# An MLP of seven block products: VectorE is held to the order in which its operations are written

## The chip, the cores and the metric

The kernel runs on one core of a Trainium2 chip. The metric is the time of one execution on the device in microseconds; what counts is the median of several runs. The hardware profiler took one execution by itself, and all rows below are from that one.

## The reference

A decoder trunk of two layers on 1024 tokens with 1024 channels, in float32. Each layer has a mixer (layer 0 gated DeltaNet, layer 1 sliding-window attention), an MLP and a gated embedding:

```python
h = h + mix
h = h + conv_ffn(rmsnorm(h, norm_ffn[i]), f_w_up[i], f_conv[i], f_w_down[i])
gate = jax.nn.sigmoid(rmsnorm(h, norm_ple[i]) @ ple_w_gate[i])
h = h + gate * (p[i] @ ple_w_proj[i])
```

The MLP, which the change is about, has 2816 hidden channels and a causal depthwise convolution with three taps behind its up projection:

```python
def conv_ffn(x, w_up, conv_w, w_down):
    u = causal_dwconv(x @ w_up, conv_w)
    gate, val = u[..., :D_FF], u[..., D_FF:]
    return (jax.nn.silu(gate) * val) @ w_down
```

## The kernel before

Channels lie on the 128 partitions and tokens along the free dimension. Every matmul operand is a pair, a rounded high part and the rest as a low part, and a product is three matmuls: high by high, low by high, high by low. All matmuls have 512 columns here, half of the tokens.

**Chunks.** `ffn` works through the hidden channels in 22 chunks j of 128. One chunk has a gate row block `z1` (tile `zg`) and a value row block `z2` (`zv`), each for two halves of the tokens. These 2 x 2 blocks are made from seven products instead of eight, in the fixed order b11, t2, t3, t1, b21, t4, b22 (`up`, L1356), each 12 matmuls. The inputs `mix.x` (b11, t12, t34, x1) are made before. The weights are sums of raw tiles: `weights` (L1240) makes s1, s2, s3 (L1252, L1253, L1255) and the second s2 (L1260) on VectorE; ScalarE rounds each to its high part (L1233) and GpSimd takes the low part (L1234). `take` (L1268) keeps four products' weights ready ahead.

The products add up in three PSUM banks of the pool `mm`: p1 (b11, then b21 on top), p7 (t3, then t4 on top), p5 (t1, then b22 on top). p6 (t2) uses the pool `d`. VectorE reads a bank between its two products, so the second has to wait for that read: `dd` = p6 - p1 (L1377), then `zv` half 1 = p7 + dd (L1394, the p7 add), minus p5 (L1397), times the row factor `rb[1]` of the norm (L1398); after b21 `zg` half 0 (L1402, L1404); after t4 `zv` half 0 (L1407, L1409); after b22 `zg` half 1 (L1416, L1418).

**Gate.** `taps` is the convolution: one operation on ScalarE (L321) and two on VectorE (L323). The value taps of chunk j follow t4 in the same chunk. `gated` (L1305), called in the chunk behind, makes the gate taps, the Silu on ScalarE (L1307), the product with the value (L1308), and by `split` its high part on ScalarE (L250, `gh`) and its low part on VectorE (L251, `gl`). Both taps read all of `z1` or `z2`, so the next chunk's p7 add, which writes into `zv`, comes behind the value taps.

In chunk 1 the row factors come into being (`nrm.factor`, `nrm.banks`), and what chunk 0 left in `zv` and `zg` is scaled by them first (L1385), so that both convolutions of chunk 0 lie in chunk 1.

**Down steps.** `step` (L1343) is a piece of the down projection: 2 x 6 matmuls on two finished chunks into two banks of the pool `d`, which has three, and two additions into an `h` tile that is loaded from DRAM beforehand and goes back there (L1340, L1350, L1351). From chunk 3 on a chunk has four steps: behind b11, behind t2, behind t4 and behind b22. Chunk 1 has none, chunk 2 has the latter two.

**Order.** The program is recorded in the order in which it is written; a scheduler then puts each engine's instructions in an order by readiness as it estimates it. `pin = tc.keep_in_program_order` exempts an instruction from that: pinned instructions of one engine keep their written order. The wrapper `E` around TensorE pins all matmuls of these stages. VectorE (`V`), ScalarE (`A`) and GpSimd (`G`) are left to the scheduler, as are the DMAs on SP's queue.

Of the kernel before, what the change touches and what calls it, by code (L numbers as in the profile page):

```python
# [9 lines left out]
F32R = mybir.dt.float32r  # L10
AF = mybir.ActivationFunctionType
ALU = mybir.AluOpType
MUL, ADD, SUB, MAX = ALU.mult, ALU.add, ALU.subtract, ALU.max
# [64 lines left out]
class Slot:  # L78
# [7 lines left out]
    def f(self):  # L86
        return self.t[:, :].bitcast(F32)
# [22 lines left out]
def kernel(  # L110
# [20 lines left out]
    out: bass.AP,  # L131
):
    nc = tc.nc
    V, A, G = nc.vector, nc.scalar, nc.gpsimd

    cp = ctx.enter_context(tc.tile_pool(name="cp", bufs=1))
    sp = ctx.enter_context(tc.tile_pool(name="sp", bufs=1))
# [5 lines left out]
    ps_ = ctx.enter_context(tc.tile_pool(name="ps", bufs=2, space=PSUM))  # L143
    S = Slots(sp, NSLOT)
    pin = tc.keep_in_program_order

    class PE:


        pinned = False  # L150
# [169 lines left out]
    def conv(dst, z, w, taps, a=0, b=T):  # L320
        A.activation(dst[:, a:b], z[:, a:b], AF.Copy, scale=w[:, 0:1])  # L321
        for i in range(1, taps):
            V.scalar_tensor_tensor(dst[:, a:b], z[:, a + i:b + i], w[:, i:i + 1], dst[:, a:b], MUL, ADD)  # L323
# [891 lines left out]
    def ffn(l, mix, nxt):  # L1215
# [72 lines left out]
        z1, z2 = S.wide("zg"), S.wide("zv")  # L1288
# [6 lines left out]
        gs = {}  # L1295
        ys = {}
        rb = []

        def taps(m, z):
            y = S.get("yf")  # L1300
            o = m * CF
            conv(y, z, fcv[:, o:o + CF], CF)
            return y

        def gated(j):  # L1305
            y1, y2 = taps(2 * j, z1), ys.pop(j)
            A.activation(y1[:, :], y1[:, :], AF.Silu)  # L1307
            V.tensor_tensor(y1[:, :], y1[:, :], y2[:, :], MUL)  # L1308
            S.put(y2)
            gs[j] = split(y1, "g")  # L1310
            S.put(y1)

        def gated_last():
# [42 lines left out]
        def up(j, early, late):  # L1356
            last = j == NF - 1

            def done(n):
                if last:  # L1360
                    mix.put(n)

            if j == 0:
                p1, p6, p7, p5 = first
                A.copy(dd, p1)
                V.tensor_tensor(dd, p6, dd, SUB)
                V.tensor_tensor(zh(z2, 1), p7, dd, ADD)
                V.tensor_tensor(zh(z2, 1), zh(z2, 1), p5, SUB)
            else:
                p1 = pmt()  # L1370
                prod(p1, *take(), "b11")
                A.copy(dd, p1)
                for _ in range(early[0]):
                    step()
                p6 = pdt()
                prod(p6, *take(), "t2")
                V.tensor_tensor(dd, p6, dd, SUB)  # L1377
                if j == 1:
                    nrm.factor()
                    p7 = pmt()  # L1380
                    prod(p7, *take(), "t3")
                    rb.extend(nrm.banks())
                    for z in (z2, z1):
                        for h in range(2):
                            V.tensor_tensor(zh(z, h), zh(z, h), rb[h], MUL)  # L1385
                        if z is z2:
                            ys[0] = taps(1, z2)
                for _ in range(early[1]):
                    step()
                gated(j - 1)  # L1390
                if j > 1:
                    p7 = pmt()
                    prod(p7, *take(), "t3")
                V.tensor_tensor(zh(z2, 1), p7, dd, ADD)  # L1394
                p5 = pmt()
                prod(p5, *take(), "t1")
                V.tensor_tensor(zh(z2, 1), zh(z2, 1), p5, SUB)  # L1397
                V.tensor_tensor(zh(z2, 1), zh(z2, 1), rb[1], MUL)  # L1398
            done("b11")
            done("t2")  # L1400
            prod(p1, *take(), "b21", first=False)
            A.copy(zh(z1, 0), p1)  # L1402
            if j:
                V.tensor_tensor(zh(z1, 0), zh(z1, 0), rb[0], MUL)  # L1404
            prod(p7, *take(), "t4", first=False)
            done("t4")
            V.tensor_tensor(zh(z2, 0), p7, dd, ADD)  # L1407
            if j:
                V.tensor_tensor(zh(z2, 0), zh(z2, 0), rb[0], MUL)  # L1409
            for _ in range(late[0]):  # L1410
                step()
            if 0 < j < NF - 1:
                ys[j] = taps(2 * j + 1, z2)
            prod(p5, *take(), "b22", first=False)
            done("b22")
            V.tensor_tensor(zh(z1, 1), p5, dd, SUB)  # L1416
            if j:
                V.tensor_tensor(zh(z1, 1), zh(z1, 1), rb[1], MUL)  # L1418
            else:
                mix.sum_squares()  # L1420
            for _ in range(late[1]):
                step()
# [54 lines left out]
        for j in range(NF):  # L1477
            n = len(todo) + len(loaded)
            if j == 2:
                load_step()  # L1480
            if j < 2 or n == 0:
                early = late = (0, 0)
            elif j == 2:
                early, late = (0, 0), (1, 1)
            elif n == 2:
                early, late = (1, 1), (0, 0)
            else:
                early, late = (1, 1), (1, 1)
            up(j, early, late)
        S.put(sa, sb)  # L1490
        hT = []
        for m in range(KT):
# [219 lines left out]
```

## Time and profile before

| what | us |
|---|---|
| median of 3 runs (2741.79 to 2749.13) | 2745.27 |
| the profiled execution | 2740.68 |
| its span from first to last instruction | 2738.8 |
| TensorE busy in the span (96%) | 2640.8 |
| VectorE busy (65%) | 1792.9 |
| GpSimd busy (43%) | 1191.4 |
| ScalarE busy (41%) | 1114.9 |

The profile gives busy time by engine, waits by the instruction that ended them, and all instructions in order of time. A matmul of 512 columns is shown with about 0.39 us, but starts come 0.23 us apart, since matmuls overlap in the pipeline; a gap in TensorE's work is therefore best read from the distance of two starts. The granted clock is TensorE's, as a share of its upper level.

### The profile page before, as it was taken

Reading aid. Unit: us, or ns where it says so; the run is one execution under the profiler, and the core shown is the slowest. Engines: PE = TensorE matmul, PEld = TensorE weight load, DVE = VectorE, ACT = ScalarE, POOL = GpSimd, SP = SyncE. Lnnn points to the kernel's source line nnn. Section 1 sums busy time; section 2 is a strip of 40 time slices with the busy share of each in tenths; the row PEclk is TensorE's granted clock in tenths of the full one; section 3 lists DMA queues with packets and bytes.
Section 4 is the critical chain, followed back from the end, with each engine's and each line's share of the span. In section 5 each row is a group of like instructions: output and inputs, shape, how many; then the busy total and the mean of one; then the engine's idle time right before and its main releaser. Section 6 shows DMA issues by size and latency. Waiting matters only on the chain. (4 is left out here: it accounts for less than half of the span.)

```text
span 2738.8 us, 35465 instructions
## 1 busy us (share of the span) xinstructions
PE 2640.8 (96%) x12914; PEld 2130.2 (78%) x12914; DVE 1792.9 (65%) x2645; ACT 1114.9 (41%) x2176; POOL 1191.4 (43%) x1132
## 2 busy tenths in 40 slices
PE   9899999999999999999999999999999999999998
PEld 7788787878777887888778776667778888888786
DVE  6555555564787777677774437775877767677745
ACT  5443443442643333333353225554533333333443
POOL 4444443442554444444532323335644444444354
PEclk9999999999999999999999999999999999999999
DMA  5222211232325555555432221122255555554323
GB/s 176 89 73 58 67 55 56 67 95 78 109 84 187 181 182 180 203 198 181 161 117 71 90 59 49 46 92 100 81 187 187 182 191 178 199 198 167 103 93 110
DMA packets 167215, 340.85 MB, mean 124 GB/s; under 512 B 38912, under 2 KB 91648, under 8 KB 167040
## 3 DMA queue, kind: packets, MB, share of 16 engines
q1 hardware_dynamic: 166176, 337.20, 37.2%
q8 instruction: 102, 1.67, 0.3%
q10 hardware_dynamic: 864, 1.38, 0.1%
q14 instruction: 73, 0.60, 0.1%
HBM read 232.56 MB, written 99.68 MB: 121 GB/s over the span
## 5 line engine op out<-in xcount | busy, mean ns | idle before, releaser
L202 POOL TENSOR_TENSOR wlo<-wraw,whi 128x512 fp32r<-128x512 f32 (+1 forms) x204 | 269.8, 1340 | 380.6 <-ACT whi L199 344.1
L153 PE MATMUL mm<-xh,whi 128*128 128x512 f32 x856 | 356.2, 416 | 3.9 <-ACT xh L255 2.8
L153 PE MATMUL mm<-xh,wlo 128*128 128x512 f32 x856 | 347.9, 406 | 0.0
L153 PE MATMUL mm<-xl,whi 128*128 128x512 f32 x856 | 346.0, 404 | 0.8 <-DVE xl L256 0.8
L212 POOL TENSOR_TENSOR dlo<-draw,dhi 128x256 fp32r<-128x256 f32 (+1 forms) x160 | 163.1, 1020 | 332.9 <-ACT dhi L211 295.7
L1234 POOL TENSOR_TENSOR wlo<-wraw,whi 128x512 fp32r<-128x512 f32 x132 | 192.6, 1466 | 147.7 <-ACT whi L1233 145.4
L1234 POOL TENSOR_TENSOR wlo<-sa,whi 128x512 fp32r<-128x512 f32 x132 | 194.1, 1470 | 141.0 <-ACT whi L1233 141.0
L153 PE MATMUL d<-gh,dhi 128*128 128x512 f32 x576 | 228.7, 397 | 4.7 <-DVE h L1350 4.2
L153 PE MATMUL d<-gl,dhi 128*128 128x512 f32 x576 | 226.9, 394 | 0.7 <-DVE gl L251 0.7
L153 PE MATMUL d<-gh,dlo 128*128 128x512 f32 x576 | 227.3, 395 | 0.0
L1350 DVE TENSOR_TENSOR h<-h,d 128x512 f32<-128x512 f32 x288 | 193.1, 680 | 32.6 <-PE d L153 32.2
L199 ACT CAST whi<-wraw 128x1024 fp32r<-128x1024 f32 (+3 forms) x122 | 100.1, 822 | 238.5 <-PE mm L153 123.4
L153 PEld LDWEIGHTS mm<-xh,wlo 128*128 128x128 f32 x856 | 163.3, 191 | 33.6 <-POOL wlo L202 0.2
L153 PEld LDWEIGHTS mm<-xh,whi 128*128 128x128 f32 x856 | 163.6, 191 | 30.6 <-ACT xh L255 3.2
L153 PEld LDWEIGHTS mm<-xl,whi 128*128 128x128 f32 x856 | 163.5, 191 | 26.9 <-DVE xl L256 1.4
L153 PE MATMUL mm<-t34h,whi 128*128 128x512 f32 x352 | 139.4, 396 | 3.7 <-DVE zv L1394 3.0
L153 PE MATMUL mm<-t34l,whi 128*128 128x512 f32 x352 | 139.6, 397 | 3.2 <-POOL t34l L919 3.2
L153 PE MATMUL mm<-x1l,whi 128*128 128x512 f32 x352 | 138.9, 395 | 0.2 <-DVE x1l L919 0.2
L153 PE MATMUL mm<-x1h,whi 128*128 128x512 f32 x352 | 138.8, 394 | 0.0
L153 PE MATMUL mm<-t34h,wlo 128*128 128x512 f32 x352 | 138.7, 394 | 0.0
L323 DVE SCALAR_TENSOR_TENSOR yf<-zv,fcv,yf 128x1024 f32<-128x1024 f32 (+1 forms) x92 | 121.5, 1321 | 26.3 <-ACT yf L321 26.2
L153 PE MATMUL mm<-x1h,wlo 128*128 128x512 f32 x352 | 138.2, 392 | 0.0
(382 smaller groups left out, 6564.0 us busy)
## 6 DMA issues: line engine op xcount, KB each, us to landing
hf<-h SPq DMA_DIRECT2D x160, 512.0 KB, 3.3
h<-hf SPq DMA_DIRECT2D x160, 512.0 KB, 4.2
wraw<-f_up SPq DMA_DIRECT2D x88, 512.0 KB, 3.3
draw<-f_down SPq DMA_DIRECT2D x144, 128.0 KB, 2.1
wraw<-a_in SPq DMA_DIRECT2D x32, 512.0 KB, 3.5
wraw<-g_w SPq DMA_DIRECT2D x24, 512.0 KB, 3.3
row<-rowd SPq DMA_DIRECT2D x16, 512.0 KB, 3.7
wraw<-b_in SPq DMA_DIRECT2D x12, 512.0 KB, 3.6
```

Source lines behind the costliest of these rows:

```text
L153: i = nc.tensor.matmul(*a, **k)
L199: A.copy(hi, raw)
L202: G.tensor_tensor(lo[:, i:j], raw[:, i:j], hi[:, i:j].bitcast(F32), SUB)
L212: G.tensor_tensor(lo, raw, hi[:, :].bitcast(F32), SUB)
L323: V.scalar_tensor_tensor(dst[:, a:b], z[:, a + i:b + i], w[:, i:i + 1], dst[:, a:b], MUL, ADD)
L1234: G.tensor_tensor(lo, src, hi.bitcast(F32), SUB)
L1350: V.tensor_tensor(t[:, hs(h)], t[:, hs(h)], ps, ADD)
```

## The change

`V` becomes a wrapper like TensorE's. While `V.pinned` is set, from chunk 1 to the end of chunk 21, each VectorE operation keeps its written place. The MLP's code is written in another order for it: `gated` is cut into three pieces, the gate taps and Silu behind b11 (in chunk 1 behind the scaling), the product and its high part behind t2, the low part behind the second step. `gated_last`, the down projection behind it and chunk 0 are not pinned.

```diff
-    V, A, G = nc.vector, nc.scalar, nc.gpsimd
+    A, G = nc.scalar, nc.gpsimd
...
+    class Vector:
+        pinned = False
+        def __getattr__(self, name):
+            f = getattr(nc.vector, name)
+            return (lambda *a, **k: pin(f(*a, **k))) if self.pinned else f
+    V = Vector()
...
-        def gated(j):
-            y1, y2 = taps(2 * j, z1), ys.pop(j)
+        def gate_taps(j):
+            y1 = taps(2 * j, z1)
             A.activation(y1[:, :], y1[:, :], AF.Silu)
+            return y1
+
+        def gate_high(j, y1):
+            y2 = ys.pop(j)
             V.tensor_tensor(y1[:, :], y1[:, :], y2[:, :], MUL)
             S.put(y2)
-            gs[j] = split(y1, "g")
+            hi = S.get("gh", F32R)
+            A.copy(hi[:, :], y1[:, :])
+            return hi
+
+        def gate_low(j, y1, hi):
+            lo = S.get("gl", F32R)
+            gs[j] = hi, lo
+            V.tensor_tensor(lo[:, :], y1[:, :], hi.f(), SUB)
             S.put(y1)
...
                 A.copy(dd, p1)
+                if j > 1:
+                    y1 = gate_taps(j - 1)
                 for _ in range(early[0]):
                     step()
...
                             ys[0] = taps(1, z2)
+                    y1 = gate_taps(0)
+                gh = gate_high(j - 1, y1)
                 for _ in range(early[1]):
                     step()
-                gated(j - 1)
+                gate_low(j - 1, y1, gh)
...
+            V.pinned = j > 0
             up(j, early, late)
+        V.pinned = False
```

Two places on VectorE, as the built programs have them. A row gives the line, the operation, and the tile written with those read. After the change every pinned row carries the wrapper's line, L154. The first place is chunk 1 of the first layer, from the scaling on. `s_6532` and `s_6537` are the row factors in PSUM, `yf_243` the value taps, `yf_244` the gate taps and then the product, `mm_6514` is p7, `mm_6561` p5, `sb` holds dd, `sa` the weight sums. Before:

```order
L1385 TENSOR_TENSOR zg_192_5916<-zg_192_5916,s_6532 128x512
L1385 TENSOR_TENSOR zg_192_5916<-zg_192_5916,s_6537 128x512
L323 SCALAR_TENSOR_TENSOR yf_243_6544<-zv_193_5917,fcv_5912,yf_243_6544 128x1024
L1260 TENSOR_TENSOR sa_190_5914<-sa_190_5914,wraw_5954 128x512
L323 SCALAR_TENSOR_TENSOR yf_243_6544<-zv_193_5917,fcv_5912,yf_243_6544 128x1024
L323 SCALAR_TENSOR_TENSOR yf_244_6550<-zg_192_5916,fcv_5912,yf_244_6550 128x1024
L1394 TENSOR_TENSOR zv_193_5917<-mm_6514,sb_191_5915 128x512
L323 SCALAR_TENSOR_TENSOR yf_244_6550<-zg_192_5916,fcv_5912,yf_244_6550 128x1024
L1397 TENSOR_TENSOR zv_193_5917<-zv_193_5917,mm_6561 128x512
L1398 TENSOR_TENSOR zv_193_5917<-zv_193_5917,s_6537 128x512
L1308 TENSOR_TENSOR yf_244_6550<-yf_244_6550,yf_243_6544 128x1024
```

With the change, in the same place:

```order
L154 SCALAR_TENSOR_TENSOR yf_243_6544<-zv_193_5917,fcv_5912,yf_243_6544 128x1024 x2
L154 TENSOR_TENSOR zg_192_5916<-zg_192_5916,s_6532 128x512
L154 TENSOR_TENSOR zg_192_5916<-zg_192_5916,s_6537 128x512
L154 SCALAR_TENSOR_TENSOR yf_244_6550<-zg_192_5916,fcv_5912,yf_244_6550 128x1024 x2
L154 TENSOR_TENSOR yf_244_6550<-yf_244_6550,yf_243_6544 128x1024
L154 TENSOR_TENSOR gl_246_6558<-yf_244_6550,gh_245_6556 128x1024
L154 TENSOR_TENSOR zv_193_5917<-mm_6514,sb_191_5915 128x512
L154 TENSOR_TENSOR zv_193_5917<-zv_193_5917,mm_6561 128x512
L154 TENSOR_TENSOR zv_193_5917<-zv_193_5917,s_6537 128x512
```

The p7 add stood ahead of the last gate tap and of the product; it now stands behind the product and the low part `gl`. The scaling of `zg` moved behind the value taps.

The second place is chunk 9 of the first layer, from the gate taps `yf` to the low part `gl`. `h_302` is the step behind b11, `h_303` (now `h_304`) the one behind t2, each emptied from two banks `d`. Before:

```order
L323 SCALAR_TENSOR_TENSOR yf_305_8376<-zg_192_5916,fcv_5912,yf_305_8376 128x1024 x2
L1350 TENSOR_TENSOR h_302_8273<-h_302_8273,d_8316 128x512
L1253 TENSOR_TENSOR sa_190_5914<-sa_190_5914,wraw_8165 128x512
L1308 TENSOR_TENSOR yf_305_8376<-yf_305_8376,yf_301_8245 128x1024
L1350 TENSOR_TENSOR h_302_8273<-h_302_8273,d_8324 128x512
L1377 TENSOR_TENSOR sb_191_5915<-d_8333,sb_191_5915 128x512
L1350 TENSOR_TENSOR h_303_8314<-h_303_8314,d_8359 128x512
L251 TENSOR_TENSOR gl_307_8383<-yf_305_8376,gh_306_8382 128x1024
```

With the change:

```order
L154 SCALAR_TENSOR_TENSOR yf_303_8308<-zg_192_5916,fcv_5912,yf_303_8308 128x1024 x2
L154 TENSOR_TENSOR h_302_8273<-h_302_8273,d_8321 128x512
L154 TENSOR_TENSOR h_302_8273<-h_302_8273,d_8329 128x512
L154 TENSOR_TENSOR sb_191_5915<-d_8338,sb_191_5915 128x512
L154 TENSOR_TENSOR yf_303_8308<-yf_303_8308,yf_301_8245 128x1024
L154 TENSOR_TENSOR h_304_8319<-h_304_8319,d_8367 128x512
L154 TENSOR_TENSOR h_304_8319<-h_304_8319,d_8375 128x512
L154 TENSOR_TENSOR gl_307_8384<-yf_303_8308,gh_305_8357 128x1024
```

The second bank of the step behind b11 was emptied after a weight sum and the product, and now right after the first; the weight sum has left this place. TensorE's order in these chunks is the same in both programs.

## Rows read from the trace of the kernel before

**Rows 1.** Stretches: us, each engine's busy us (instructions), PEclk, DMA share, GB/s.

```profile
786.00:1384.00 598.00, 594.11 (x2551) 477.94 (x2550) 440.04 (x526) 216.90 (x335) 278.35 (x211) 1.00 0.53 180
1960.00:2558.00 598.00, 596.51 (x2566) 480.65 (x2565) 437.61 (x528) 216.37 (x333) 270.17 (x209) 1.00 0.52 180
```

**Rows 2.** TensorE's waits: waiting line <- releaser: us in total, times, longest.

```profile
PE d L153 <- DVE h L1350: 4.2, 5, 1.5
...
PE mm L153 <- DVE zv L1394: 3.0, 2, 1.5
```

**Rows 3.** TensorE in order of time, t4: start, us, instruction, count [idle before].

```profile
785.17 0.50 PE L153 MATMUL mm<-t34h,whi 128*128 128x512 f32 x1 [1.51 <-DVE zv L1394]
...
804.74 0.40 PE L153 MATMUL mm<-t34h,whi 128*128 128x512 f32 x1
...
1958.69 0.50 PE L153 MATMUL mm<-t34h,whi 128*128 128x512 f32 x1 [1.47 <-DVE zv L1394]
```

**Rows 4.** TensorE in order of time, down steps of the first layer.

```profile
826.37 0.50 PE L153 MATMUL d<-gh,dhi 128*128 128x512 f32 x1 [0.63 <-DVE h L1350]
...
1010.43 0.40 PE L153 MATMUL d<-gh,dlo 128*128 128x512 f32 x1
1010.95 0.50 PE L153 MATMUL d<-gh,dhi 128*128 128x512 f32 x1
1011.29 0.39 PE L153 MATMUL d<-gl,dhi 128*128 128x512 f32 x1
1011.52 0.39 PE L153 MATMUL d<-gh,dlo 128*128 128x512 f32 x1
...
1321.73 0.50 PE L153 MATMUL d<-gh,dhi 128*128 128x512 f32 x1 [1.55 <-DVE h L1350]
```

**Rows 5.** VectorE in order of time, chunk 9 of the first layer.

```profile
1005.42 0.68 DVE L1350 TENSOR_TENSOR h<-h,d 128x512 f32<-128x512 f32 x1
1007.96 1.21 DVE L1253 TENSOR_TENSOR sa<-sa,wraw 128x512 f32<-128x512 f32 x1 [1.85 <-POOL wlo L1234]
1009.09 1.21 DVE L1308 TENSOR_TENSOR yf<-yf,yf 128x1024 f32<-128x1024 f32 x1
1010.23 0.67 DVE L1350 TENSOR_TENSOR h<-h,d 128x512 f32<-128x512 f32 x1
```

**Rows 6.** VectorE in order of time, chunk 1 of the first layer.

```profile
777.72 1.29 DVE L1385 TENSOR_TENSOR zv<-zv,s 128x512 f32<-128x512 f32 x2 [2.47 <-PE s L157]
...
780.24 1.28 DVE L323 SCALAR_TENSOR_TENSOR yf<-zv,fcv,yf 128x1024 f32<-128x1024 f32 x1
...
784.43 0.69 DVE L1394 TENSOR_TENSOR zv<-mm,sb 128x512 f32<-128x512 f32 x1
...
787.98 1.22 DVE L1308 TENSOR_TENSOR yf<-yf,yf 128x1024 f32<-128x1024 f32 x1
...
790.32 1.23 DVE L251 TENSOR_TENSOR gl<-yf,gh 128x1024 fp32r<-128x1024 f32 x1
```

**Rows 7.** ScalarE in order of time, the same chunk.

```profile
779.04 1.16 ACT L321 ACTIVATE yf<-zv,fcv 128x1024 f32<-128x1024 f32 x1 [0.80 <-DVE zv L1385]
...
786.78 1.06 ACT L1307 ACTIVATE yf<-yf 128x1024 f32<-128x1024 f32 x1 [2.11 <-DVE yf L323]
...
789.24 1.05 ACT L250 CAST gh<-yf 128x1024 fp32r<-128x1024 f32 x1 [0.92 <-DVE yf L1308]
```

**Rows 8.** Stretches behind two idle times of TensorE, columns as in rows 1.

```profile
130.70:136.00 5.30, 5.29 (x40) 5.00 (x41) 2.59 (x4) 0.00 (x0) 0.00 (x0) 1.00 0.09 35
...
430.70:436.00 5.30, 5.30 (x21) 4.91 (x22) 2.05 (x3) 1.05 (x1) 0.00 (x0) 0.50 0.00 0
```

**Rows 9.** TensorE in order of time, the starts of those stretches and the second's end.

```profile
130.71 1.02 PE L153 MATMUL d<-R,A 128*128 128x128 f32 x7 [3.67 <-DMA R<-xd]
...
430.69 3.75 PE L153 MATMUL d<-R,A 128*128 128x128 f32 x16 [6.05 <-DMA R<-xd]
...
435.10 0.63 PE L153 MATMUL mm<-xh,whi 128*128 128x512 f32 x1
435.52 0.61 PE L153 MATMUL mm<-xl,whi 128*128 128x512 f32 x1
```

## The prediction

> **What bounds the kernel now.** I read the table of stretches first, then TensorE's waits, then the order of time around each wait. From 786 to 1384 us and from 1960 to 2558 us, where chunks 2 to 20 of the two MLPs run, TensorE is without work for 598.00 - 594.11 = 3.9 us and 598.00 - 596.51 = 1.5 us [rows 1]. So the MLP is bound by TensorE's own pace, and only its stops can be won. Two kinds of stop name VectorE [rows 2].
>
> The first is the start of t4 in chunk 1, once in each layer: TensorE waits 1.51 and 1.47 us for `zv` L1394 [rows 3]. That is the read of bank p7, on top of which t4 goes on adding.
>
> The second comes in every other chunk, at the second down step, where a matmul into `d` waits for a bank that L1350 has still to empty. In the first layer there are nine such places, one per two chunks, the first at 826.37 and the last at 1321.73 us [rows 4]; in the second layer I count nine too. Idle time shows only a part of one: at 1010.43 the next matmul comes 0.52 us later and the one after it 0.34 us, where the pace is 0.23 [rows 4], so this stop takes 0.40 us. Against 0.12 us of visible idle (0.52 less the matmul's 0.40) about 0.27 us per stop is hidden. The stops together are at most 3.9 + 1.5 + 18 x 0.27 = 10.3 us.
>
> **The change, part by part.** No instruction is added or taken away; only places change. The sum starts from the profiled execution, 2740.7 us, which is 4.6 us (0.17%) below the median of the runs.
>
> *Stops of the steady chunks.* Before, VectorE emptied one half of the first step at 1005.42, waited 1.85 us for GpSimd ahead of the weight sum L1253, made that, made the gate product L1308, and only at 1010.23 emptied the other half [rows 5]. Now both emptyings stand ahead of the product, and the weight sum stands after the t1 product of the chunk. A bank is then free some 3 us before it is asked for: the emptying takes 0.68 us [rows 5], and a product of TensorE lasts 2.80 us (seven lie between 785.17 and 804.74 [rows 3]). I take 10 us off; the bounds are 5 (half of the stops find another cause) and 10.3. The tap operations stay ahead of these emptyings, and VectorE is busy 440.04 of 598 us [rows 1], so what is late next is nothing on this path in chunks 3 to 20. The DMA loads of `h` that an emptying needs and the stores behind it keep their step of lead on SP's queue; I cost them at nothing, under that cover (if it goes, see the third rival).
>
> *Chunk 1.* Here the new order works against the change. The p7 add, which t4 waits for, stands behind the whole gate of chunk 0: four row scalings, two convolutions, the Silu, the product and its high and low parts. Before, the scheduler had put it after three of the four taps. The start is the same, since at 777.72 VectorE waits for the row factors in PSUM [rows 6]. From there, by durations of this trace: `zv` scaled 1.29, its tap on ScalarE 1.16, two taps 2 x 1.28, `zg` scaled as `zv` 1.29, its tap 1.16, two taps 2.56, Silu 1.06, product 1.22, high part 1.05, low part 1.23, add 0.69 [rows 6, 7]. That is 15.3 us, an end at 793.0 instead of 784.43 + 0.69 = 785.12. TensorE's order is fixed too, so t4 starts 7.9 us later than at 785.17, after an idle stretch of 9.4 us instead of 1.51. ScalarE can't shorten it: each of its steps takes in what VectorE has just made.
>
> *What the idle stretch does to the clock.* After 6.05 us without work TensorE ran on at a granted clock of 0.50, the lower of its levels, until 436 us, with matmuls 0.42 us apart; after 3.67 us without work it ran on at 1.00 [rows 8, 9]. 9.4 us lies nearer the first. The lower level lasted 5.3 us from the restart there. Of that, t4's twelve matmuls at 0.42 instead of 0.23 make up to 2.3 us; I take 2.0, between 0 (clock kept) and 2.3. [...]
>
> *Chunk 2.* VectorE now comes out of chunk 1 late: p5 subtracted, scaled, two weight sums, `zg` scaled, a third sum, six operations of about 0.7 us, end near 797.2. t4 ends at 793.0 + 2.8 + 2.0 = 797.8. From there VectorE and ScalarE have the same chain again: p7 add and scaling 1.3, tap and taps 3.7, `zg` 1.3, tap and taps 3.7, Silu, product, high, low part 4.6, a weight sum 0.7, p7 add 0.7, together 16.0, an end at 813.8 [rows 5, 6, 7]. TensorE has six products between, 16.8 us, and starts t4 of chunk 2 at 814.6. So nothing is lost in chunk 2 by itself: it starts 814.6 - 804.74 = 9.9 us late [rows 3]. With the clock kept VectorE would be last, at 797.2 + 16.0 + 0.05 = 813.3, or 8.5 us late; with 2.3 us it is 10.2. From chunk 3 on the steps' products give VectorE its slack back.
>
> *The last chunk* has no steps, and the p7 add comes behind the gate once more, but with its taps begun a chunk earlier. I reckon the add within 1 us of t4's turn, and cost it 0, at most 1 us a layer. The second layer's chunk 1 has the same wait (1.47 us) and the same code, so all counts twice.
>
> **Sum.** 2740.7 + 2 x 9.9 - 10 = 2750.5 us for the profiled execution. On the median, 2745.3 + 9.8, that is 2755 us. Ends of the costs: 2 x 8.5 - 10.3 = +6.7, and 2 x (10.2 + 1) - 5 = +17.4.
>
> **Rivals.** *First, faster.* The stops go and chunk 1 doesn't grow. It is decided by one point: when the p7 add of chunk 1 ends. Every microsecond of it counts twice, and the ten of the stops are used up when t4 starts 5 us later than now; if it starts before 786 us the kernel is near 2737. For it speaks that the add itself needs only `dd`, p7 and the end of the `zv` taps; against it, that its place on VectorE is fixed behind the low part, and the chain ahead has no two steps that could overlap. Even a gate in half the time would leave 2 x 4 us.
>
> *Second, no difference that can be told.* By about 0.3%, 8 us, a measurement of this kernel can tell a change from none. The clock stays up, as it did after 3.67 us [rows 8, 9], and all stops go: 2 x 8.5 - 10.3 = +6.7, 2752 us. Part of the forecast's own spread falls here too. For it speaks the row at 130.71, against it the one at 430.69.
>
> *Third, slower by more.* A strict queue makes every wait everybody's wait. If an emptying meets a load of `h` that is late, or the low part meets a slot that a store still reads, the steps behind it are late as well, and TensorE stops in each chunk. In rows 5 a wait of 1.85 us on GpSimd already stands in VectorE's way without stopping TensorE by more than 0.40. At 0.5 to 1 us in each of 36 chunks it would be +18 to +36 on top of 2 x 9.9, near 2785. Against it: VectorE has 158 us of slack in 598 [rows 1], and the loads are issued a step ahead.
>
> That the pinning doesn't take hold is excluded, since VectorE's order as built shows it, in chunks 1 to 21 of both layers.
>
> **How the numbers follow.** The forecast with its spread, slower by over 8 us: 0.55, and the third rival 0.08, so 0.63 for slower. The second, with the low end of the forecast: 0.31 for within 0.3%. The first: 0.06. The likeliest time is 2755. The range takes in the costs' ends (2752 to 2763) and some 4 us for the spread of the runs: 2747 to 2767, which leaves out the first rival and the third.
>
> **What would show it.** In the changed profile: t4 of chunk 1 should start near 793.0 and 1966.5 us, with an idle stretch over 9 us named after VectorE's add; the granted clock should read 0.5 for some microseconds behind it; t4 of chunk 2 should start near 814.6; the waits for L1350's emptyings (all pinned VectorE work carries one line, that of the wrapper) should be gone from TensorE's list; TensorE's idle in chunks 3 to 20 should fall under 1 us a layer. I am wrong if t4 of chunk 1 waits less than 5 us more, or if TensorE stops in the steady chunks.

## The result, and the profile after

The changed kernel takes 2755.72 us (median of 6 runs, 2753.48 to 2758.69), the kernel before 2746.79 us in the same session (6 runs, 2741.79 to 2750.42). The ratio is 1.0033, with a 95% interval from 1.0022 to 1.0043: slower by 6 to 12 us. The profiled execution took 2756.19 us, with a span of 2754.5 us.

First the table of stretches of the changed kernel, columns as in [rows 1]: the two stretches of [rows 1], then the first layer from the row factors of chunk 1 to the start of t4 in chunk 2, and 4.4 us from the start of t4 in chunk 1 on.

```profile
786.00:1384.00 598.00, 587.90 (x2526) 476.09 (x2527) 467.20 (x525) 211.98 (x332) 287.90 (x210) 0.99 0.51 177
1960.00:2558.00 598.00, 587.03 (x2522) 474.89 (x2521) 466.77 (x526) 212.33 (x330) 286.83 (x208) 0.99 0.51 175
779.10:817.70 38.60, 27.55 (x113) 21.66 (x111) 29.06 (x30) 14.00 (x18) 11.60 (x8) 0.87 0.09 29
...
794.60:799.00 4.40, 4.40 (x11) 3.49 (x12) 4.27 (x6) 1.24 (x2) 1.59 (x2) 0.54 0.39 119
```

The same way from the factors to t4 of chunk 2 in the kernel before:

```profile
777.70:804.70 27.00, 25.49 (x112) 20.45 (x111) 26.84 (x30) 14.29 (x19) 13.02 (x9) 1.00 0.22 67
```

The two rows from the factors to that t4 hold the loss. VectorE (the third busy time) does 30 operations in both. Before, they fill 26.84 of 27.0 us. Now the stretch takes 38.6 us, VectorE works 29.06 of it and is idle for 9.5. The loss of 11.6 us is 9.4 of idle time and 2.2 of busy time. Of the 2.2, longer operations make 0.7 (the durations of the 30 add up to 29.30 us before and 29.98 now); the rest comes from the records of successive operations, which overlap by 2.02 us before and by 0.90 now, and from 0.44 us of the last operation before, which lie behind the stretch.

TensorE's waits of the changed kernel, as in [rows 2]:

```profile
PE mm L164 <- DVE zv L154: 24.2, 6, 9.5
```

The wait for the `zv` adds has grown from 3.0 to 24.2 us, and the wait for emptied `d` banks is gone from the list. TensorE in order of time shows four of the six places; the other two are 1.48 us in chunk 2 and 1.10 in chunk 21 of the second layer:

```profile
794.55 0.80 PE L164 MATMUL mm<-t34h,whi 128*128 128x512 f32 x1 [9.50 <-DVE zv L154]
795.15 0.63 PE L164 MATMUL mm<-t34l,whi 128*128 128x512 f32 x1
795.58 0.63 PE L164 MATMUL mm<-t34h,wlo 128*128 128x512 f32 x1
...
799.31 0.39 PE L164 MATMUL mm<-x1h,whi 128*128 128x512 f32 x1
...
817.69 0.50 PE L164 MATMUL mm<-t34h,whi 128*128 128x512 f32 x1 [1.55 <-DVE zv L154]
...
1389.82 0.50 PE L164 MATMUL mm<-t34h,whi 128*128 128x512 f32 x1 [1.07 <-DVE zv L154]
...
1971.79 0.80 PE L164 MATMUL mm<-t34h,whi 128*128 128x512 f32 x1 [9.49 <-DVE zv L154]
```

Chunk 1 waits 9.5 us where it waited 1.5 [rows 3]; behind it matmuls start 0.43 us apart (795.15 to 795.58), at a granted clock of 0.54 from 794.6 to 799 us, close to the 0.50 of [rows 8]. The row at 799.31 is the first matmul of b22: t4's twelve took 4.76 us. Chunks 2 and 21 have a wait that they had not had. VectorE in order of time, chunks 1 and 2 of the first layer, answers to [rows 6]:

```profile
779.08 1.29 DVE L154 TENSOR_TENSOR zv<-zv,s 128x512 f32<-128x512 f32 x2 [2.57 <-PE s L168]
781.59 2.60 DVE L154 SCALAR_TENSOR_TENSOR yf<-zv,fcv,yf 128x1024 f32<-128x1024 f32 x2 [1.22 <-ACT yf L332]
784.11 1.28 DVE L154 TENSOR_TENSOR zg<-zg,s 128x512 f32<-128x512 f32 x2
786.61 2.61 DVE L154 SCALAR_TENSOR_TENSOR yf<-zg,fcv,yf 128x1024 f32<-128x1024 f32 x2 [1.22 <-ACT yf L332]
790.34 1.23 DVE L154 TENSOR_TENSOR yf<-yf,yf 128x1024 f32<-128x1024 f32 x1 [1.12 <-ACT yf L1318]
792.67 1.22 DVE L154 TENSOR_TENSOR gl<-yf,gh 128x1024 fp32r<-128x1024 f32 x1 [1.11 <-ACT gh L1326]
793.82 0.68 DVE L154 TENSOR_TENSOR zv<-mm,sb 128x512 f32<-128x512 f32 x1
...
799.51 0.69 DVE L154 TENSOR_TENSOR zv<-mm,sb 128x512 f32<-128x512 f32 x1 [0.27 <-PE mm L164]
800.24 0.69 DVE L154 TENSOR_TENSOR zv<-zv,s 128x512 f32<-128x512 f32 x1
802.14 3.52 DVE L154 SCALAR_TENSOR_TENSOR yf<-zv,fcv,yf 128x1024 f32<-128x1024 f32 x2 [1.22 <-ACT yf L332]
...
808.22 3.52 DVE L154 SCALAR_TENSOR_TENSOR yf<-zg,fcv,yf 128x1024 f32<-128x1024 f32 x2 [1.22 <-ACT yf L332]
...
816.95 0.69 DVE L154 TENSOR_TENSOR zv<-mm,sb 128x512 f32<-128x512 f32 x1
```

Each bracket that names ACT is a hand-over in which VectorE stands still while ScalarE makes a tap, the Silu or the high part. Four of them in chunk 1 make 4.67 us. In [rows 6] no row after the first has a bracket: the scheduler put other work into those times. The second `zv` add of these rows (799.51), the one behind t4, waited 0.27 us for TensorE, so TensorE is hardly the late one in chunk 2. The last row (816.95) is the p7 add that t4 of chunk 2 waits for.

### The profile page after: what moved, and what is told of

Its sections match the earlier page's. It is cut to its first block, busy times and chain, and to the rows that moved or that the text cites. A ratio compares the mean times of both kernels' runs of the same rounds, so it can differ in the third digit from the quotient of the medians.

```text
span 2754.5 us, 35439 instructions
## 1 busy us (share of the span) xinstructions
PE 2642.7 (96%) x12914; PEld 2138.5 (78%) x12914; DVE 1848.7 (67%) x2645; ACT 1110.3 (40%) x2176; POOL 1218.9 (44%) x1132
## 4 chain that ended last, share of the span: by engine, by line
PE 62%; DVE 8%; ACT 2%; issue 1%; POOL 1%; DMA 0%; DVEq 0%; POOLq 0%; ACTq 0%
PE mm L164 35%; PE d L164 25%; PE s L164 2%; DVE yf L154 2%; DVE sc L1108 1%; PE d L168 1%; DVE sc L1084 1%; ACT yf L332 0%; ACT sc L1101 0%; DVE zv L154 0%; DVE zg L154 0%; DVE h L902 0%; DVE sq L980 0%; DVE gl L154 0%; POOL wlo L213 0%
## 5 line engine op out<-in xcount | busy, mean ns | idle before, releaser
L223 POOL TENSOR_TENSOR dlo<-draw,dhi 128x256 fp32r<-128x256 f32 (+1 forms) x160 | 202.7, 1268 | 292.3 <-ACT dhi L222 292.3
L1245 POOL TENSOR_TENSOR wlo<-sa,whi 128x512 fp32r<-128x512 f32 x132 | 172.1, 1312 | 216.2 <-ACT whi L1244 216.2
L1245 POOL TENSOR_TENSOR wlo<-wraw,whi 128x512 fp32r<-128x512 f32 x132 | 208.7, 1588 | 125.1 <-ACT whi L1244 125.1
L154 DVE TENSOR_TENSOR h<-h,d 128x512 f32<-128x512 f32 x288 | 193.1, 682 | 36.8 <-PE d L164 32.4
L164 PEld LDWEIGHTS mm<-xh,whi 128*128 128x128 f32 x856 | 163.5, 191 | 30.6 <-ACT xh L266 3.2
L164 PEld LDWEIGHTS mm<-xl,whi 128*128 128x128 f32 x856 | 163.9, 191 | 26.9 <-DVE xl L267 1.4
L164 PE MATMUL mm<-t34h,whi 128*128 128x512 f32 x352 | 141.8, 403 | 25.4 <-DVE zv L154 24.2
L1244 ACT CAST whi<-wraw 128x512 fp32r<-128x512 f32 x132 | 79.7, 620 | 158.3 <-PE mm L164 97.3
L1244 ACT CAST whi<-sa 128x512 fp32r<-128x512 f32 x132 | 79.9, 619 | 156.6 <-PE mm L164 86.0
L154 DVE SCALAR_TENSOR_TENSOR yf<-zv,fcv,yf 128x1024 f32<-128x1024 f32 x84 | 135.7, 1616 | 10.4 <-ACT yf L332 8.9
L154 DVE SCALAR_TENSOR_TENSOR yf<-zg,fcv,yf 128x1024 f32<-128x1024 f32 x84 | 123.9, 1474 | 27.2 <-ACT yf L332 25.2
```

The costliest lines, as they stand in the source:

```text
L154: return (lambda *a, **k: pin(f(*a, **k))) if self.pinned else f
L164: i = nc.tensor.matmul(*a, **k)
L223: G.tensor_tensor(lo, raw, hi[:, :].bitcast(F32), SUB)
L1244: A.copy(hi, src)
L1245: G.tensor_tensor(lo, src, hi.bitcast(F32), SUB)
```

## The experiments

Every kernel is read by the same anchors: F, the last transposition of the row factors in chunk 1, and the first matmul of t4 in chunks 1, 2, 3, 20 and 21. The table gives the distances in us, first layer / second layer. "MLPs" is the time from F to the row factors of the gated embedding, both layers together, and "ratio" goes against runs of the kernel before on the same chip.

| kernel | median, ratio [95%] | F to t4(1) | F to t4(2) | t4(2) to t4(3) | t4(3) to t4(20) | t4(20) to t4(21) | MLPs |
|---|---|---|---|---|---|---|---|
| before | 2746.8 | 7.3 / 7.3 | 26.9 / 26.9 | 31.5 / 32.4 | 526.2 / 521.9 | 19.6 / 19.5 | 1342.9 |
| before_again | one run, 2746.8 | 7.3 / 7.3 | 26.9 / 26.9 | 31.6 / 32.4 | 525.7 / 523.3 | 19.6 / 19.5 | 1346.7 |
| after | 2755.7, 1.0033 [1.0022, 1.0043] | 15.3 / 15.3 | 38.5 / 38.6 | 30.7 / 30.7 | 520.5 / 520.4 | 20.9 / 21.0 | 1358.8 |
| e1 | 2763.5, 1.0055 [1.0035, 1.0074] | 5.8 / 5.8 | 38.5 / 38.5 | 32.3 / 33.0 | 520.5 / 520.4 | 21.0 / 21.0 | 1363.6 |
| e2 | 2747.7, 0.9992 [0.9979, 1.0006] | 5.8 / 5.8 | 31.0 / 31.0 | 34.7 / 33.2 | 520.5 / 521.5 | 19.5 / 19.6 | 1349.9 |
| e3 | 2741.1, 0.9970 [0.9957, 0.9982] | 7.9 / 7.9 | 29.8 / 30.1 | 30.7 / 30.7 | 520.5 / 520.4 | 21.0 / 21.0 | 1341.2 |
| e4 | 2761.5, 1.0046 [1.0033, 1.0058] | 15.4 / 15.4 | 37.7 / 38.9 | 33.8 / 33.8 | 523.0 / 522.9 | 19.5 / 19.5 | 1364.6 |
| e5 | 2738.6, 0.9968 [0.9955, 0.9980] | 7.3 / 7.3 | 26.9 / 26.9 | 31.7 / 31.8 | 522.6 / 522.6 | 19.5 / 19.5 | 1336.8 |
| e7 | 2763.5, 1.0057 [1.0035, 1.0078] | 15.4 / 15.4 | 38.6 / 38.6 | 32.3 / 33.2 | 520.5 / 520.4 | 21.0 / 21.0 | 1364.1 |
| e8 | 2734.7, 0.9949 [0.9930, 0.9968] | 7.3 / 7.3 | 26.9 / 26.9 | 30.6 / 31.0 | 520.5 / 520.4 | 19.5 / 19.5 | 1331.9 |
| e10 | 2730.8, 0.9935 [0.9916, 0.9955] | 6.3 / 6.3 | 25.8 / 25.8 | 31.3 / 30.6 | 520.5 / 520.4 | 19.5 / 19.5 | 1330.6 |
| e11 | 2883.1, 1.0489 [1.0472, 1.0505] | 7.3 / 7.3 | 26.9 / 26.9 | 31.8 / 32.3 | 588.0 / 589.1 | 20.7 / 19.6 | 1477.3 |
| e12 | 2761.2, 1.0060 [1.0044, 1.0076] | 15.4 / 15.4 | 38.6 / 38.6 | 30.7 / 30.7 | 520.5 / 520.4 | 20.9 / 21.0 | 1359.2 |

What lies outside the MLPs took 1393.7 to 1402.3 us in these executions, in no order that the edits explain. A few microseconds between two medians are therefore read from the MLP columns.

**e1: only the p7 add moved ahead, in chunk 1.**

```diff
                             ys[0] = taps(1, z2)
+                            V.tensor_tensor(zh(z2, 1), p7, dd, ADD)
...
-                V.tensor_tensor(zh(z2, 1), p7, dd, ADD)
+                if j > 1:
+                    V.tensor_tensor(zh(z2, 1), p7, dd, ADD)
```

> The changed kernel with one VectorE operation moved: in chunk 1 the p7 add stands directly behind the value taps, ahead of chunk 0's gate; the p5 subtraction stays behind the gate. My theory (the p7 add's place costs the 8.0 us per layer): t4 of chunk 1 starts without a wait, within 1 us of where TensorE is ready, about 6 us after the row factors instead of 15.4. The wait moves on to b22 of chunk 1, which needs the read of p5 behind the gate: TensorE stands there for some 4 us. Net, t4 of chunk 2 comes 2 to 4 us earlier than in the changed kernel in each layer: 2747 to 2752 us, 4 to 8 us under the changed kernel. Rival (VectorE's total of work from the factors to chunk 2 decides, wherever the add stands): t4 of chunk 2 comes at the same time as in the changed kernel, 2755 to 2757 us, though t4 of chunk 1 is early.

TensorE in order of time, chunk 1 and 2 of the first layer:

```profile
784.88 0.50 PE L164 MATMUL mm<-t34h,whi 128*128 128x512 f32 x1
...
795.27 0.77 PE L164 MATMUL mm<-x1h,whi 128*128 128x512 f32 x1 [7.34 <-DVE zv L154]
...
817.59 0.50 PE L164 MATMUL mm<-t34h,whi 128*128 128x512 f32 x1 [4.04 <-DVE zv L154]
```

The rival was right about the place. t4 of chunk 1 starts without a wait, 9.6 us earlier than in the changed kernel, and nothing comes of it: b22 waits 7.34 us instead, and t4 of chunk 2 starts 38.5 us after F as before the edit. VectorE's strict chain through both chunks sets that time, not the place of one add in it. The time was over both forecasts, 6.5 us over the rival's 2757. Part of it stands behind the 4.04 us wait: there the granted clock fell (0.79 from 820 to 825 us), and from t4 of chunk 2 to t4 of chunk 3 it takes 1.6 and 2.3 us more than in the changed kernel.

**e2: a better strict order, by hand.** In chunks 1, 2 and 21 the p7 add and the p5 subtraction stand ahead of the gate product; in chunk 1 all scalings come first.

```diff
+                    ys[0] = taps(1, z2)
+                    V.tensor_tensor(zh(z2, 1), p7, dd, ADD)
+                    p5 = pmt()
+                    prod(p5, *take(), "t1")
+                    V.tensor_tensor(zh(z2, 1), zh(z2, 1), p5, SUB)
...
+                bare = early == (0, 0)
+                if not bare:
+                    gh = gate_high(j - 1, y1)
...
+                if bare:
+                    gh = gate_high(j - 1, y1)
...
+                if bare:
+                    gate_low(j - 1, y1, gh)
```

> Pinned as in the changed kernel, but in the chunks without down steps ahead of t4 (1, 2 and 21) the p7 add and the p5 subtraction stand ahead of the gate product; in chunk 1 all four scalings come first, then the value taps, the p7 add, the p5 subtraction, and only then the gate taps. My theory (only the places in these chunks cost; the pinning as such gains the 10 us of the steady chunks): t4 of chunk 1 starts about 6 us after the factors with a wait under 0.5 us, t4 of chunk 2 and of chunk 21 without a wait over 0.5 us, no stop in chunks 3 to 20; 8 + 3.65 + 1.5 us per layer less than the changed kernel, so 20 to 26 us less: 2730 to 2737 us, which is 10 to 17 us under the kernel before. Rival (pinning costs something in VectorE's other work, as the 56 us of added VectorE time suggest): 2745 us or more, no gain on the kernel before.

Over both layers it gains 15.1 us on the changed kernel up to t4 of chunk 2, loses 6.5 from there to t4 of chunk 3 and gains 2.9 in chunk 21; against the kernel before there is no difference. TensorE has new waits in the first layer, these the longest:

```profile
796.90 0.51 PE L164 MATMUL d<-t12h,wlo 128*128 128x512 f32 x1 [2.09 <-POOL wlo L1245]
...
817.12 0.50 PE L164 MATMUL d<-gl,dhi 128*128 128x512 f32 x1 [2.14 <-DVE gl L154]
```

Whatever I put behind the gate became late in its turn: the weight sums, which GpSimd turns into low parts, and the low part `gl`, which the first down step reads. The forecast of 2730 to 2737 was wrong. The rival's time, 2745 or more, came true, but hardly by a cost of pinning in all chunks: chunks 3 to 20 keep their gain in the first layer and all but 1.2 us of it in the second, and what was lost lies between t4 of chunk 2 and t4 of chunk 3.

**e3, e8, e5, e4: what pinning costs or gains in which chunks.** All but e8 are the code of the change with another condition; e8 also writes the gate of chunks 1, 2 and 21 in one piece, as before the change.

```diff
-            V.pinned = j > 0
+            V.pinned = j > 1              # e3
+            V.pinned = sum(early) == 2    # e8, chunks 3 to 20
+            V.pinned = False              # e5
+            V.pinned = (j == 1)           # e4
```

> The changed kernel with chunk 1 left to the scheduler; pinned from chunk 2 on. My theory: chunk 1 as before the change (t4 waits about 1.5 us), chunk 2 no later than before by more than 2 us, the stops of the steady chunks gone as in the changed kernel: 10 us less than before, plus up to 1.5 us per layer in chunk 21, 2737 to 2742 us. Rival (the gain in the steady chunks only seems one, because VectorE comes into them late and TensorE's stops fell into the idle stretch of chunk 1): 2746 us or more.

> Pinned only in chunks 3 to 20, where the new order holds four steps; in chunks 1, 2 and 21 the gate is written in one piece as before the change and VectorE is left to the scheduler. My theory: the chunks with steps gain from the pinned order, the chunks without lose because a strict order leaves VectorE idle while ScalarE works on the gate; so chunks 1, 2 and 21 are as before (7.3 us to t4 of chunk 1, then 19.6 to t4 of chunk 2, 19.5 from chunk 20 to 21), chunks 3 to 20 as after (520.4 us): 2733 to 2738 us, 4 to 7 us under the version that is pinned from chunk 2 on. Rival (pinned chunks need a pinned start: coming out of the scheduler's chunk 2, the stops return): 2741 us or more.

> The code in the new written order, but VectorE left to the scheduler in all chunks. Theory A (the pinning does it, the writing alone nothing): chunks 1 and 2 as before the change within 1 us, stops in chunks 3 to 20 as before: within 4 us of the kernel before. Theory B (the new writing already gives the scheduler a better order in the steady chunks): chunks 3 to 20 at 520 to 522 us in both layers, 2735 to 2740 us.

> The new written order, pinned in chunk 1 alone; chunks 2 to 21 are left to the scheduler. The same writing without any pin ran at 2738.6 us. My theory (the strict order of chunk 1 costs by itself): t4 of chunk 1 at 15.3 us after the factors as in the changed kernel, 8.0 us later than unpinned, in each layer; chunk 2, no longer strict, fills VectorE's waits and may make up a part of the lateness or none: 2738.6 + 2 x (5 to 10) = 2749 to 2759 us, with chunk 21 at 19.5 us. Rival (the strict chunk 2 is what carries the lateness on; a free one takes it back, since TensorE is late itself): t4 of chunk 2 at 27 to 29 us after the factors, 2739 to 2743 us.

The time of e3 came where it was expected, 2741.1 us. In it t4 of chunk 2 still comes 3 us late, where I had allowed 2, and chunk 21 costs its 1.5. e8 has chunks 1, 2 and 21 as before and chunks 3 to 20 as after: 2734.7 us. e4 shows the loss alone: with chunk 1 the only pinned one, t4 of chunk 1 is as late as in the changed kernel, and the free chunk 2 takes back 0.8 us in the first layer and nothing in the second. Behind it even chunk 3 is 2 us longer than in e5; 2761.5 us is 2.5 over the range that I gave. e5 is the surprise. The new writing alone, with the scheduler free, brings chunks 3 to 20 to 522.6 us in both layers and the kernel to 2738.6. So theory B of that run holds nearly to the end (0.6 us over its bound), and what pinning adds between t4(3) and t4(20) is some 2 us a layer (522.6 to 520.5 and 520.4). Against the first profile of the kernel before, what the writing gains from t4(2) to t4(20) lies in the first layer alone (3.4 us, and nothing in the second). Another 2.7 us of its gain lies behind chunk 21, in the down projection, and no run shows its cause.

**e11: the old writing, pinned in chunks 3 to 20.**

> The old written order (the whole gate in one piece behind the second step), pinned in chunks 3 to 20 only. Theory A (a strict order gains only if it is written as TensorE delivers): the gate taps and all the gate now stand behind the emptyings of the second step, and the p7 add behind the gate; from the second step's end the gate takes 8.3 us by the rows of the kernel before (tap 1.16, taps 2.56, Silu 1.06, product 1.22, high 1.05, low 1.23) and the add 0.7, TensorE has three products, 8.4 us, so it stops 0.6 us or more in each of 18 chunks, up to 3 us where taps take 3.5 us and not 2.6: 2755 to 2840 us in all. Theory B (the strict order itself is what gains, by emptying the banks in turn): 2735 to 2745 us.

TensorE's waits of the whole kernel:

```profile
PE mm L164 <- DVE zv L154: 98.5, 36, 5.4
```

One of them in order of time:

```profile
1082.14 0.80 PE L164 MATMUL mm<-t34h,whi 128*128 128x512 f32 x1 [4.65 <-DVE zv L154]
1082.73 0.63 PE L164 MATMUL mm<-t34l,whi 128*128 128x512 f32 x1
1083.16 0.63 PE L164 MATMUL mm<-t34h,wlo 128*128 128x512 f32 x1
```

There are 36 waits, as many as such chunks, 2.7 us in the mean. My expectation of up to 3 us each holds for the mean alone: in the first layer waits of about 1.1 us take turns with waits of about 4.7, and the longest, in the second layer, is 5.4. t4(3) to t4(20) takes 65.5 and 66.5 us more than in e5, 132 together, and the kernel 43 us more than the upper end. The waits make 98.5 of the 132. Behind a long wait the matmuls start 0.43 us apart again, and that I had left out; how much of the other 33 us it makes, no run separates. A strict order is only as good as the order that is written.

**e7 and e12: is it the clock?** e7 fills the gap in chunk 1 with 40 matmuls that nobody reads; e12 also puts 14 ahead of t4 in chunk 2.

```diff
-            prod(p1, *take(), "b21", first=False)
+            wb, = take()
+            prod(p1, wb, "b21", first=False)
...
+            if j == 1:                    # e12: j in (1, 2), 40 and 14
+                busy = pdt()
+                for _ in range(40):
+                    E.matmul(busy, ch(wb[0], 0), mix.x["t4"][0][0], start=True, stop=True)
             prod(p7, *take(), "t4", first=False)
```

> The changed kernel with 40 more matmuls of 512 columns into a spare bank, recorded ahead of t4 of chunk 1 in both layers; nobody reads what they make. At 0.23 us each they fill 9.2 us of the 9.9 us in which TensorE has nothing to do. Theory A (VectorE's chain alone sets the start of t4 in chunk 2): the granted clock stays at 1.00 there, t4 of chunk 1 starts where it did, the matmuls of t4 come 0.23 us apart instead of 0.43, and t4 of chunk 2 starts at most 0.5 us earlier, after a longer wait of 3 to 4 us: 2754 to 2757 us. Theory B (the 2.0 us of my clock term count): t4 of chunk 2 starts 2 us earlier in each layer, 2750 to 2752 us.

> The version with 40 filler matmuls in chunk 1's gap, and 14 more of them (3.2 us at 0.23) ahead of t4 of chunk 2, where that version waited 3.5 us for the p7 add and then ran t4 and what follows at a lower granted clock. Nobody reads what they make. Theory A (the 7.7 us which the first filler added to the changed kernel come from the clock falling in the second wait, where TensorE and not VectorE is last): the clock stays at 1.00 from t4 of chunk 2 on, t4 of chunk 2 comes at 38.5 us after the factors again, from it to t4 of chunk 3 30.7 us and not 32.3 and 33.2, 2757 to 2761 us. Theory B (the filler itself costs, by what it takes from other engines or by the clock of later stages): 2763 us or more again.

TensorE's start of t4 in chunk 2 of e7:

```profile
817.77 0.51 PE L164 MATMUL mm<-t34h,whi 128*128 128x512 f32 x1 [3.50 <-DVE zv L154]
```

The table of stretches of e7, chunk 2 and what follows (the granted clock is the third number from the end):

```profile
815.00:820.00 5.00, 2.23 (x8) 1.81 (x9) 4.49 (x7) 1.36 (x3) 1.29 (x1) 0.91 0.49 175
820.00:825.00 5.00, 5.00 (x18) 3.94 (x17) 3.89 (x6) 2.30 (x5) 3.65 (x3) 0.75 0.09 34
```

and of e12:

```profile
815.00:820.00 5.00, 4.72 (x21) 3.55 (x20) 4.77 (x8) 0.81 (x2) 1.29 (x1) 1.00 0.60 210
820.00:825.00 5.00, 5.00 (x23) 4.05 (x23) 4.93 (x7) 3.55 (x6) 4.49 (x4) 1.00 0.00 0
```

In e7 the clock stays up in chunk 1 (1.00 in every stretch from 785 to 815 us), t4 of chunk 1 starts at the same time (794.54) and runs 12 matmuls at 0.23 us, and t4 of chunk 2 starts 38.6 us after F, as ever. So theory A of e7 holds for that anchor: the 2.0 us of my clock term weren't on the path. Its time, 2754 to 2757 us, was missed by 6.5 us. But TensorE's time went into a longer wait in chunk 2 (3.50 us), the clock fell there (0.75 from 820 to 825 us), and the later matmuls of t4 and the first of the step behind it start 0.40 to 0.43 us apart (819.04 to 822.43): 1.6 and 2.5 us more to t4 of chunk 3. e12 keeps the clock in both waits (1.00 in every stretch from 780 to 830 us) and has 30.7 us again, and its MLPs take what those of the changed kernel take. The runs as a whole don't tell e7 and e12 apart (1.0057 and 1.0060): that the clock made the difference is shown in the traces alone.

**before_again: a second profile of the kernel before.**

> The kernel before once more, for a second profiled execution. Between the two profiled executions the change cost 15.5 us, between the medians 8.9. Theory A: the steady stops of the kernel before differ from execution to execution, and the first profile caught few of them; then this one, if it is nearer the median, has more than the 5.7 and 1.4 us of stops in chunks 3 to 20 that the first showed over the 520.4 us of the changed kernel, 3 to 7 us more in the two layers, with the same chunks 1 and 2. Theory B: the executions differ outside the MLP (the mixers); then the MLPs take the same 1343 us again within 1.5.

This execution is 6.1 us longer than the first. Chunks 1 and 2 are the same; chunks 3 to 20 hold only 0.9 us more, the down projection behind chunk 21 of the second layer 2.8 us, and 2.3 us lie outside the MLPs. Neither theory holds by itself. Against this execution the change costs 9.4 us, near the 8.9 of the medians.

**e10: a version that beats both.** e8, and in chunk 1 the value taps, the p7 add and the gate taps are written in this order and pinned, only those five. In chunks 2 and 21 the p7 add is written ahead of the gate as well, but the scheduler is free there.

```diff
+                    V.pinned = True
+                    ys[0] = taps(1, z2)
...
                 V.tensor_tensor(zh(z2, 1), p7, dd, ADD)
+                if not full:
+                    y1 = gate_taps(j - 1)
+                    V.pinned = False
```

> As the version pinned in chunks 3 to 20 only, and in chunk 1 five VectorE operations keep a written order: both value taps, the p7 add, both gate taps; in the kernel before the first gate tap stood ahead of the p7 add. My theory: the add comes one tap, 1.2 us, earlier, so t4 of chunk 1 waits 0.3 us instead of 1.5, and chunk 2 keeps its pace: 1.2 us per layer less than the version pinned in chunks 3 to 20 only, some 2.4 us in all. Rival (VectorE's chain through chunks 1 and 2 sets t4 of chunk 2, as it did when the p7 add alone was moved): t4 of chunk 2 not earlier than 26.9 us after the factors, no difference.

```profile
784.35 0.51 PE L164 MATMUL mm<-t34h,whi 128*128 128x512 f32 x1 [0.45 <-DVE zv L154]
```

The wait of t4 in chunk 1 falls from 1.5 to 0.45 us and, other than in e1, t4 of chunk 2 comes 1.1 us earlier too: the rival is out. The ratio to the kernel before is 0.9935 [0.9916, 0.9955], some 17 us faster, and the best of all. Against e8 it isn't settled: the intervals overlap, and the MLPs differ by 1.3 us, less than expected.

## Why the prediction was right, and where its steps were not

**Time and sign were right**: 2755 forecast, 2755.7 measured, inside the range. The places were right too: t4 of chunk 1 after 15.3 us from F (my chain: 793.0 - 777.72 = 15.3), an idle stretch of 9.5 us (9.4), a granted clock of 0.54 behind it, no wait left for the steps' banks, and no idle time of TensorE from 818 to 1388 us.

*Steady chunks, -10 forecast.* The columns from t4(2) to t4(20) give -2.5 - 7.2 = -9.7 us. The size is right, but by e5 not all of it is the strict order's: without any pin, the new writing alone takes 3.3 us off these columns, a third of it. That is from one profile each; between the two profiles of the kernel before these columns differ by 1.0 us.

*Chunk 1, +7.9 per layer.* Measured +8.0. The step holds as worked out.

*The clock, +2.0 per layer.* The price was right, the place wrong. t4's twelve matmuls took 4.76 us (794.55 to 799.31) where they took 2.9 in e7, so 1.9 more: nine starts lay 0.42 us or more apart, the last three 0.23 to 0.28. But the prediction let this time pass through TensorE to t4 of chunk 2. There TensorE wasn't last: VectorE waited only 0.27 us for it (799.51), and e7, with the clock kept at 1.00, starts that t4 at the same 38.6 us.

*Chunk 2, no wait of its own, 9.9 us late.* This step failed. t4(2) came 38.5 - 26.9 = 11.6 and 11.7 us late, and with a wait. VectorE's chain took 817.64 - 799.51 = 18.1 us instead of 16.0. What was mis-sized is the chain: I had taken 1.28 us for a tap from [rows 6], the length that taps have there with GpSimd all but idle (0.12 us of work from 780.24 to 784.22); here two taps took 3.52 us instead of 2.56, twice, beside a busy GpSimd (2.91 of 3.6 us from 802.1 on, 1.89 of 3.5 from 808.2 on; last section). That is 1.9 of the 2.1 us. The trace of the kernel before had such taps already (two in 3.13 us, at 793.38), and I passed over them.

*Last chunk, 0, at most 1.* Measured +1.4 and +1.5. A weight sum and the whole gate stand ahead of the add there. It is the strict order that costs this: e5, with the same writing and no pin, has 19.5 us.

By these, the sum is 2 x 11.65 - 9.7 + 2.9 = +16.5 instead of +9.8, and profile against profile it is +15.5. The medians differ by 8.9 only. So it was luck that the median came out within a microsecond of the forecast: the parts were 6.7 us short, and the execution that I started from was itself a short one (2740.7 against 2746.8 for the second), so that the two errors cancelled. My upper end, +17.4, covered the parts.

*The rivals.* The first gave one deciding point, the end of the p7 add, with 2737 us if t4 starts before 786. e1 starts it at 784.88 and takes 2763.5: the point was wrong, since what counts is the next anchor that all of chunk 1's work must pass. The second didn't happen; the clock fell to 0.54. The third didn't in the changed kernel, but e11 has its stop in every chunk, 36 waits, from pins in chunks 3 to 20 with the old writing; they are waits for the p7 add, not for emptied banks or loads. (Its price was added up too low: 2745.3 + 19.8 + 18 to 36 is 2783 to 2801, and I wrote near 2785.)

## What to carry to other kernels

Pin an engine only where the written order keeps it full: where two engines handed one chain back and forth, in chunk 1, the strict order turned four hand-overs into 4.67 us of idle time, and the scheduler had filled them. Judge a moved operation at the next point that everything must pass, not at the wait it removes; e1 removed 9.5 us of one wait and gained nothing. And try a rewritten order without the pin first: here it gave 0.32% of the 0.51% that the pin in the right chunks came to (the intervals of e5 and e8 overlap; that e8 is the faster one rests on the columns of the table).

## What the runs showed of the hardware

Some of VectorE's operations became slower and some faster, with as many of them as before. Groups of VectorE's operations from 860 to 1360 us in the kernel before (count, busy us, mean ns):

```profile
L1350 DVE TENSOR_TENSOR h<-h,d 128x512 f32<-128x512 f32 x130 | 87.1, 680 | 13.6 <-PE d L153 13.4
L323 DVE SCALAR_TENSOR_TENSOR yf<-zv,fcv,yf 128x1024 f32<-128x1024 f32 x32 | 41.0, 1281 | 9.4 <-ACT yf L321 9.4
...
L1253 DVE TENSOR_TENSOR sa<-sa,wraw 128x512 f32<-128x512 f32 x16 | 22.2, 1389 | 18.6 <-POOL wlo L1234 18.6
L1260 DVE TENSOR_TENSOR sa<-sa,wraw 128x512 f32<-128x512 f32 x16 | 19.9, 1246 | 16.6 <-POOL wlo L1234 16.6
...
L1255 DVE TENSOR_TENSOR sb<-wraw 128x512 f32<-128x512 f32 x16 | 11.2, 699 | 0.0
```

and in the changed kernel:

```profile
L154 DVE TENSOR_TENSOR h<-h,d 128x512 f32<-128x512 f32 x131 | 88.0, 682 | 17.6 <-PE d L164 15.5
L154 DVE SCALAR_TENSOR_TENSOR yf<-zv,fcv,yf 128x1024 f32<-128x1024 f32 x32 | 51.2, 1600 | 0.6
...
L154 DVE TENSOR_TENSOR sa<-sa,wraw 128x512 f32<-128x512 f32 x32 | 26.9, 841 | 1.9 <-DVE sa L154 0.5
L154 DVE TENSOR_TENSOR sb<-wraw 128x512 f32<-128x512 f32 x16 | 26.5, 1654 | 0.0
```

The weight sum `sb`, with two inputs in SBUF, went from 699 to 1654 ns, the value taps from 1281 to 1600. The sums `sa`, also with two inputs in SBUF, went the other way, from 1389 and 1246 to 841. The emptying, with one input in PSUM, stayed nearly as it was (680 and 682). What goes on beside them is GpSimd making low parts of the weights. In this stretch of the kernel before, an `sa` sum took 692 ns in the mean with nothing on GpSimd beside it and 1526 with something; in the changed kernel 689 and 1230. The emptying took 678 to 685 either way. GpSimd of the changed kernel in order of time, in chunk 2:

```profile
800.37 1.30 POOL L1245 TENSOR_TENSOR wlo<-sb,whi 128x512 fp32r<-128x512 f32 x1
802.79 4.03 POOL L1245 TENSOR_TENSOR wlo<-wraw,whi 128x512 fp32r<-128x512 f32 x2 [1.12 <-ACT whi L1244]
808.77 1.89 POOL L1245 TENSOR_TENSOR wlo<-wraw,whi 128x512 fp32r<-128x512 f32 x1 [1.95 <-ACT whi L1244]
```

VectorE and GpSimd of the kernel before, in its chunk 2:

```profile
793.38 3.13 DVE L323 SCALAR_TENSOR_TENSOR yf<-zv,fcv,yf 128x1024 f32<-128x1024 f32 x2
...
791.55 2.56 POOL L1234 TENSOR_TENSOR wlo<-wraw,whi 128x512 fp32r<-128x512 f32 x2 [3.64 <-ACT whi L1233]
```

Beside the two taps at 802.14 (3.52 us instead of the 2.60 of chunk 1) two low parts take 4.03 us; one with no such operation beside it, at 800.37, took 1.30. So both took longer in these rows. No run took GpSimd's work away, so that this is the cause is read from such rows and not tested. The overlap isn't new either: two taps took 3.13 us at 793.38 in the kernel before. In the changed kernel it falls on other operations and there is more of it (from 860 to 1360 us VectorE's operations lie beside GpSimd's for 174.5 us before and for 198.6 now): VectorE's busy time grows from 1792.9 to 1848.7 us. In the steady chunks that costs nothing that shows: TensorE is busy for 570.00 of the 570.00 us from 818 to 1388. In chunk 2 the four taps took 7.0 us a layer, 1.9 more than in my chain; in the first layer of the kernel before they took 6.1.

The granted clock was 1.00 behind the changed kernel's waits of 1.07 to 1.55 us, and fell behind one of 3.50 us in e7 (0.75 from 820 to 825 us), while it stayed at 1.00 behind 3.67 us in the kernel before [rows 8, 9]. In this case, then, a wait's length alone doesn't foretell the clock.
